# Two first-layer pieces instead of one in each pair of output tiles of an interleaved feed-forward, one Trainium2 core

## The chip, the core and the metric

The kernel runs on one core of a Trainium2 chip. Its engines run side by side, each through its own queue in order: TensorE (matmuls, PE in the profile), VectorE (DVE), ScalarE (ACT), GpSimd (POOL) and SyncE (SP), which issues the loads. The metric is the time of one execution in device microseconds; the time before is the median of three runs.

## The reference

One layer of a hybrid backbone over 1024 tokens of width 1024: a modulated RMSNorm, an input projection into four head groups (convolution, Fourier mixing, neighbourhood attention, state space), an output projection, and then the feed-forward, where the change lies:

```python
def squared_relu_mlp(h, w1, b1, w2, b2):
    return jnp.square(jax.nn.relu(h @ w1 + b1)) @ w2 + b2

hx = modulate(rmsnorm(x_mid, g_norm_mlp[l]), sh2, sc2)
x = x_mid + gt2 * squared_relu_mlp(hx, w_ff1[l], b_ff1[l], w_ff2[l], b_ff2[l])
return rmsnorm(x, g_final)
```

`w_ff1` is 1024 x 4096, `w_ff2` is 4096 x 1024, all in float32.

## The kernel before, in words

Matrices are kept transposed, tokens in two halves of 512. Each float32 operand is split into a high and a low part; a product of 128 x 128 weights with 128 x 512 data takes three matmuls (`mm3w`, line 1470): high by high, high by low, and third the low weights by high. The weights' high part is made by ScalarE, the low part by GpSimd (`w_split`, lines 1455 and 1456).

The 4096 hidden rows are done in 16 units of 256. Both layers use a Strassen-like scheme with seven products where a plain one has eight. For the first layer of unit `u` the seven products are called a11, a12, s1, s2, s3, s4, a22; each has two halves, the 14 *pieces* of six matmuls (`a11.0`, `a11.1` and so on below). They gather in three PSUM banks: qa (a11, s2, s3, a22), qb (s1, s4) and qc (a12). After certain pieces their bank is read: a11.1 copies qa into tile 11, a12.1 adds qc and applies relu and square (`more`, line 1627), s1.1 copies qb into 22, s2.1 copies qa into 12, s3.1 adds qa to 22, s4.1 adds qb to 12 (this add is called `more(12)` below), a22.1 starts 21. Then `sums` (lines 1636 to 1638) and `sum_21` (1645) combine the tiles, and `part` splits them for the second layer (`h_split`: ScalarE the high part, VectorE the low part, line 1488). The sums of the weights for s1 to s4 are made by VectorE (lines 1605, 1607, 1609, 1611).

The second layer of unit `u-1` has four *pairs* of output tiles, each with seven products of three matmuls: a0, a1, b1, b0, c0, c1 and d, where d is run in the next pair, behind its a1. Each product is followed by an add into the result X on VectorE (`add_x`, line 1493). a0, b0, c1 and d of a pair use one bank (fa, of which there are two), one after the other, so each of them waits for the add of the one before; b1 and c0 share fb, a1 uses fc. The weights of a pair are loaded into one of two buffers and combined there by GpSimd (lines 1704 to 1708, three operations right behind the split of `a`, one behind that of `b`); the next load into the buffer is issued with the split of `d`.

The order of the work is written out. `pair_pieces(u - 1, q)` puts pieces of unit `u` between the products of unit `u-1`; three pieces stand ahead of the first pair, and what is left of the 14 comes behind the last, as the unit's tail. `Pieces.emit` walks through that list: at each position it first emits the preparation (split, sums, loads) of what stands up to five positions ahead, then the matmuls, then the callbacks that are due:

```python
            for i, (k, mm, post) in enumerate(self.seq):
                while keys and at[keys[0]] <= i + ahead:
                    key = keys.pop(0)
                    self.w[key] = self.prep[key]()
                mm(self.w[k])
                for d, fn in enumerate(post or ()):
                    self.due.setdefault(i + d, []).append(fn)
                for fn in self.due.pop(i, ()):
                    fn()
```

Within this block TensorE, ScalarE, GpSimd and VectorE run what they are given in that order (`MAN`, line 1447); SyncE's loads and the work outside of the block are placed by a planner. The unit ahead of the paired ones (`u` = 2) is interleaved with `plain_pieces`, which has no such pairs and isn't changed.

Of the kernel before, what the change touches and what calls it, by code (L numbers as in the profile page):

```python
# [49 lines left out]
def body(tc, A, out, dbg=None):  # L50
# [39 lines left out]
    def ps_tile(tag, name, n=512):  # L90
        return cur["pool"].tile([P, n], F32, name=name, tag=tag, bufs=cur["tags"][tag])
# [1359 lines left out]
    def w_split(a):  # L1451

        n = a.shape[1]
        hi, lo = [wf.tile([P, 2, P], F32R, name=s, tag=s, bufs=6)[:, :n] for s in ("w2h", "w2l")]
        S.activation(hi, a, AF.Copy)  # L1455
        G.tensor_tensor(lo, a, hi.bitcast(F32), ALU.subtract)  # L1456
        return hi, lo

    def w1_load(f, i):
        r = wf.tile([P, 4, P], F32, name="w1r", tag="w1r", bufs=4)  # L1460
        SP.dma_start(r, A["w_ff1"][f, :, 4 * i:4 * i + 4])
        return r
# [7 lines left out]
    def mm3w(o, w, i, m, start, stop):  # L1470
        for j, (a_, m_) in enumerate(((w[0], m[0]), (w[0], m[1]), (w[1], m[0]))):
            PE.matmul(o, a_[:, i, :], m_, start=start and j == 0, stop=stop and j == 2, skip_group_check=True)  # L1472

    def f_tile():
        return fin.tile([P, H], F32, name="ft", tag="ft", bufs=4)

    def act(t, f, src=None):

        S.activation(t, t if src is None else src, AF.Relu, bias=CF("b_ff1", f))
        S.activation(t, t, AF.Square)  # L1480

    def h_split(t, extra=False):
        if extra:
            hi, lo = [th_p.tile([P, H], F32R, name=s, tag=s, bufs=3) for s in ("th", "tl")]
        else:
            hi, lo = [fin.tile([P, H], F32R, name=s, tag=s, bufs=4) for s in ("fh", "fl")]
        S.activation(hi, t, AF.Copy)  # L1487
        V.tensor_tensor(lo, t, hi.bitcast(F32), ALU.subtract)  # L1488
        return hi, lo
# [86 lines left out]
    pc = Pieces()  # L1576
# [5 lines left out]
    def q_pieces(u):  # L1582

        ts, d = {}, {}
        units[u] = d
        st = {}

        def load(i):
            if u + 1 < NU2:
                raws.setdefault(u + 1, []).append(w1_load(2 * u + 2 + i // 2, i % 2))  # L1590

        def bank(tag):
            if tag not in st:
                st[tag] = ps_tile(tag, tag)
            return st[tag]

        def prep(name, h):
            def fn():
                a11, a12, a21, a22 = raws[u]
                if h == 0 and name == "s1":  # L1600
                    st["ws"] = wf.tile([P, 4, P], F32, name="ws", tag="ws", bufs=1)
                ws = st.get("ws")
                if h == 0:
                    if name == "s1":
                        ES.tensor_tensor(ws, a21, a22, ALU.add)  # L1605
                    elif name == "s2":
                        ES.tensor_tensor(ws, ws, a11, ALU.subtract)
                    elif name == "s3":
                        ES.tensor_tensor(a21, a11, a21, ALU.subtract)  # L1609
                    elif name == "s4":  # L1610
                        ES.tensor_tensor(ws, a12, ws, ALU.subtract)
                a = {"a11": a11, "a12": a12, "a22": a22, "s3": a21}.get(name, ws)
                w = w_split(a[:, 2 * h:2 * h + 2])
                if h == 0 and name == "s4":
                    for i in range(3):
                        load(i)
                if h == 1 and name == "a22":
                    load(3)
                return w
            return fn  # L1620

        def new(i, bank_):
            ts[i] = f_tile()
            S.copy(ts[i], bank_)  # L1624

        def more(i, bank_, also=None):
            V.tensor_tensor(ts[i], ts[i], bank_, ALU.add)
            if also:
                also()
            act(ts[i], 2 * u + i // 20)  # L1630

        def part(key, i, extra=False):
            d[key] = h_split(ts[i], extra)

        def sums():
            V.tensor_tensor(ts[11], ts[12], ts[11], ALU.subtract)
            V.tensor_tensor(ts[12], ts[22], ts[12], ALU.subtract)
            V.tensor_tensor(ts[22], ts[22], ts[11], ALU.subtract)

        def begin_21():  # L1640
            ts[21] = f_tile()
            act(ts[21], 2 * u + 1, st["qa"])

        def sum_21():
            V.tensor_tensor(ts[21], ts[21], ts[22], ALU.subtract)

        post_q1 = (lambda: new(11, st["qa"]),)
        post_q2 = (lambda: more(11, st["qc"]),)
        post_q5 = (lambda: new(22, st["qb"]),)
        post_q6 = (lambda: new(12, st["qa"]),)  # L1650
        pre_q7 = (lambda: part((0, 0), 11),)
        post_q7 = (lambda: more(22, st["qa"]),)
        if u == NU2 - 1:
            post_q3 = (lambda: more(12, st["qb"]), lambda: part((1, 1), 22), lambda: part((0, 1), 12))
            post_q4 = (begin_21, lambda: part((1, 0), 21))
        else:
            post_q3 = (lambda: more(12, st["qb"], lambda: part((1, 1), 22)), sums)
            post_q4 = (lambda: (begin_21(), part("t1", 11)), lambda: (part((1, 0), 21), part("t2", 22, True)),
                       lambda: (sum_21(), part("t3", 12, True)), lambda: part("t4", 21, True))

        def piece(name, tag, b, start, h, post):
            def mm(w):
                o = bank(tag)
                for k in range(2):
                    mm3w(o, w, k, b[2 * h + k], start and h == 0 and k == 0, h == 1 and k == 1)
            pc.entry((u, name, h), prep(name, h))
            return lambda: pc.add((u, name, h), mm, post if h == 1 else pre_q7 if name == "s3" else None)

        return [piece(*x[:4], h, x[4]) for x in (
            ("a11", "qa", b11, True, post_q1), ("a12", "qc", b21, True, post_q2), ("s1", "qb", c1, True, post_q5),  # L1670
            ("s2", "qa", c2, False, post_q6), ("s3", "qa", c3, False, post_q7), ("s4", "qb", b22, False, post_q3),
            ("a22", "qa", c4, False, post_q4)) for h in range(2)]
# [18 lines left out]
    def pair_pieces(u, q):  # L1691

        late = []
        for p in range(4):
            g = 4 * u + p
            k0, k1 = 2 * p, 2 * p + 1
            bk = {}

            def prep(name, g=g):
                def fn():  # L1700
                    t = raw2[g]
                    w = w_split({"a": t[:, 0:2], "b": t[:, 0:5:4], "c": t[:, 1:3], "d": t[:, 3:4]}[name])
                    if name == "a":
                        EP.tensor_tensor(t[:, 4], t[:, 2], t[:, 3], ALU.add)
                        EP.tensor_tensor(t[:, 2], t[:, 0], t[:, 2], ALU.subtract)
                        EP.tensor_tensor(t[:, 0], t[:, 4], t[:, 0], ALU.subtract)  # L1706
                    elif name == "b":
                        EP.tensor_tensor(t[:, 1], t[:, 1], t[:, 0], ALU.subtract)
                    if name == "d":
                        raw2_load(g + 2)  # L1710
                    return w
                return fn

            for name in "abcd":
                pc.entry((u, p, name), prep(name))

            def prod(name, i, tag, key, hf, k, start, bk=bk, p=p):
                def mm(w):
                    if start:
                        bk[tag] = ps_tile(tag, tag)  # L1720
                    mm3w(bk[tag], w, i, units[u][key], start, True)
                return lambda: pc.add((u, p, name), mm, (lambda: add_x(hf, k, bk[tag]),))

            prod("a", 0, "fa", (0, 0), 0, k0, True)()
            if p == 0:
                q.pop(0)()
            prod("a", 1, "fc", (1, 0), 0, k0, True)()
            if late:
                late.pop()()
            prod("b", 1, "fb", "t1", 1, k1, True)()  # L1730
            prod("b", 0, "fa", "t2", 1, k0, False)()
            q.pop(0)()
            prod("c", 0, "fb", (1, 1), 1, k0, False)()
            prod("c", 1, "fa", "t3", 1, k1, False)()
            late.append(prod("d", 0, "fa", "t4", 0, k1, False))
        q.pop(0)()
        late.pop()()
# [30 lines left out]
    with tc.manual_schedule(engines=MAN):  # L1768
        for u in range(2, NU2):
            q = q_pieces(u)  # L1770
# [164 lines left out]
```

## Time and profile before

| | us |
|---|---|
| median of three runs | 1342.34 (1338.53 to 1344.2) |
| the profiled execution | 1341.13 |
| its span | 1339.0 |
| TensorE busy (matmuls) | 1197.4 (89%) |
| VectorE busy | 1068.4 (80%) |
| GpSimd busy | 808.6 (60%) |
| ScalarE busy | 652.7 (49%) |

The span runs from the first to the last instruction of the profiled execution; its time has 2.1 us more around it. Busy times overlap. The feed-forward's paired units lie between about 770 and 1290 us of the span. TensorE's matmuls are pipelined, so what one takes is read from the distance of two starts, and their shown lengths overlap.

### The profile page before, as it was taken

To read this page: it belongs to the slowest core of one execution; us is meant where nothing else is said; L and a number is where in the kernel's file an instruction comes from. 1 tells how busy PE (TensorE), PEld (TensorE's weight loads), DVE (VectorE), ACT (ScalarE), POOL (GpSimd) and SP (SyncE) were. 2 spreads that over 40 slices of the span, in tenths; PEclk is the share of its full clock that TensorE was granted. 3 is DMA by queue.
4 is the path that set the end of the run, shared out by engine and by line. 5 is a ranking of instruction groups with operands and counts; after the bars stand their busy time and mean duration, and the time that the engine had idled before them with its cause. 6 is when DMAs were issued, how large, how long until landed. Compare 5 with 4: busy or idle time off the path is not lost.

```text
span 1339.0 us, 18718 instructions
## 1 busy us (share of the span) xinstructions
PE 1197.4 (89%) x6188; PEld 965.5 (72%) x6188; DVE 1068.4 (80%) x1636; ACT 652.7 (49%) x1337; POOL 808.6 (60%) x1002
## 2 busy tenths in 40 slices
PE   5889878898865999899999999999999999999996
PEld 3657656777655777777778777777877777777775
DVE  4775999869999768658695579888888888888867
ACT  5254333323446565554664445555545555444555
POOL 3825677372556734015367477777877778787754
PEclk9989898998975999898999999999999999999998
DMA  9455232161153544323121121111211112211113
GB/s 344 142 164 164 81 125 79 47 199 66 51 177 94 175 128 142 109 78 143 32 77 43 40 64 32 48 56 56 63 56 32 52 52 63 64 41 39 56 40 126
DMA packets 75058, 121.77 MB, mean 91 GB/s; under 512 B 16977, under 2 KB 35154, under 8 KB 74962
## 3 DMA queue, kind: packets, MB, share of 16 engines
q1 hardware_dynamic: 62802, 113.24, 26.9%
q10 hardware_dynamic: 12160, 7.34, 1.8%
q8 instruction: 49, 0.80, 0.3%
q14 instruction: 47, 0.39, 0.1%
HBM read 106.68 MB, written 13.88 MB: 90 GB/s over the span
## 4 chain that ended last, share of the span: by engine, by line
PE 48%; DVE 29%; ACT 5%; issue 4%; POOL 4%; DMA 3%; SPq 1%; ACTq 0%; DVEq 0%; POOLq 0%
PE fa L1472 11%; PE qa L1472 6%; PE qb L1472 5%; PE fb L1472 5%; DVE cacc L1015 5%; DVE tl L1488 3%; PE fc L1472 2%; DVE fl L1488 2%; PE f L1472 2%; PE p_t L1270 2%; PE mm L1097 2%; PE mm L1472 2%; DVE Ss L698 2%; DVE Ss L697 1%; DVE X L1493 1%
## 5 line engine op out<-in xcount | busy, mean ns | idle before, releaser
L1456 POOL TENSOR_TENSOR w2l<-w2r,w2h 128x128 fp32r<-128x128 f32 (+1 forms) x232 | 177.4, 766 | 75.3 <-ACT w2h L1455 68.1
L1493 DVE SCALAR_TENSOR_TENSOR X<-fa,gt2c,X 128x512 f32<-128x512 f32 x216 | 159.4, 745 | 13.0 <-PE fa L1472 13.0
L1455 ACT ACTIVATE w2h<-w2r 128x128 fp32r<-128x128 f32 (+1 forms) x232 | 85.8, 387 | 150.8 <-POOL w2r L1706 79.8
L1456 POOL TENSOR_TENSOR w2l<-w1r,w2h 128x256 fp32r<-128x256 f32 x136 | 108.5, 814 | 57.7 <-ACT w2h L1455 34.0
L235 POOL TENSOR_TENSOR wlo<-wraw,whi 128x1024 fp32r<-128x1024 f32 x30 | 75.2, 2508 | 102.0 <-ACT whi L233 82.9
L1493 DVE SCALAR_TENSOR_TENSOR X<-fb,gt2c,X 128x512 f32<-128x512 f32 x108 | 80.5, 745 | 35.4 <-PE fb L1472 35.3
L1456 POOL TENSOR_TENSOR w2l<-ws,w2h 128x256 fp32r<-128x256 f32 x84 | 67.9, 815 | 41.4 <-ACT w2h L1455 40.1
L1015 DVE SCALAR_TENSOR_TENSOR cacc<-cv,wdw,cacc 128x512 f32<-128x512 f32 x92 | 92.3, 1047 | 0.6
L364 PE MATMUL mm<-xl,whi 128*128 128x512 f32 x192 | 81.2, 424 | 3.8 <-DVE xl L220 3.8
L364 PE MATMUL mm<-xh,whi 128*128 128x512 f32 x192 | 77.3, 423 | 7.0 <-ACT xh L218 5.8
L1472 PE MATMUL fa<-th,w2h 128*128 128x512 f32 x156 | 63.2, 405 | 19.7 <-DVE X L1493 19.7
L364 PE MATMUL mm<-xh,wlo 128*128 128x512 f32 x192 | 80.6, 420 | 0.0
L1455 ACT ACTIVATE w2h<-w1r 128x256 fp32r<-128x256 f32 x136 | 53.9, 409 | 47.5 <-DVE w1r L1609 16.5
L1472 PE MATMUL qa<-cb,w2h 128*128 128x512 f32 x224 | 70.7, 397 | 0.7 <-ACT ft L1624 0.7
L1488 DVE TENSOR_TENSOR fl<-ft,fh 128x512 fp32r<-128x512 f32 x64 | 56.9, 906 | 12.8 <-ACT fh L1487 12.7
L1472 PE MATMUL fa<-th,w2l 128*128 128x512 f32 x156 | 61.7, 396 | 0.6 <-POOL w2l L1456 0.6
L1472 PE MATMUL fa<-tl,w2h 128*128 128x512 f32 x156 | 61.5, 394 | 0.0
L1013 POOL TENSOR_TENSOR pacc<-pacc,ptmp 128x512 f32<-128x512 f32 x24 | 37.4, 1559 | 29.8 <-ACT ptmp L1012 29.8
L1455 ACT ACTIVATE w2h<-ws 128x256 fp32r<-128x256 f32 x84 | 33.1, 410 | 42.4 <-DVE ws L1605 20.4
L1472 PEld LDWEIGHTS fa<-th,w2h 128*128 128x128 f32 x156 | 29.3, 188 | 30.8 <-DVE X L1493 25.2
L364 PEld LDWEIGHTS mm<-xh,whi 128*128 128x128 f32 x192 | 38.1, 201 | 18.4 <-ACT xh L218 7.2
L1472 PEld LDWEIGHTS qa<-cb,w2h 128*128 128x128 f32 x224 | 42.0, 188 | 11.2 <-ACT ft L1624 1.1
(788 smaller groups left out, 3945.3 us busy)
## 6 DMA issues: line engine op xcount, KB each, us to landing
w2r<-in_w_ff SPq DMA_DIRECT2D x68, 256.0 KB
wmB<-in_wmodB SPq DMA_DIRECT2D x32, 512.0 KB
w1r<-in_w_ff SPq DMA_DIRECT2D x64, 256.0 KB
wm<-in_wmodA SPq DMA_DIRECT2D x16, 512.0 KB
wraw<-in_w_in SPq DMA_DIRECT2D x12, 512.0 KB
x<-in_xT SPq DMA_DIRECT2D x8, 512.0 KB
wraw<-in_w_out SPq DMA_DIRECT2D x8, 512.0 KB
kr<-k_d SPq DMA_DIRECT2D x16, 256.0 KB
```

Source lines behind the costliest of these rows:

```text
L235: (lo_eng or G).tensor_tensor(lo, raw, hi.bitcast(F32), ALU.subtract)
L364: PE.matmul(o, a_[:, k, :], b_[hf][k], start=k == 0 and i == 0, stop=k == 7 and i == 2)
L698: V.tensor_tensor_scan(Ss[b_, i, g, ::-1], r_[b_], src[b_, g, ::-1], 0.0, ALU.mult, ALU.add)
L1013: G.tensor_tensor(pacc, pacc, t, ALU.add)
L1015: V.scalar_tensor_tensor(acc, x(k), w(k), acc, ALU.mult, ALU.add)
L1097: PE.matmul(o, a_[:, 2 * kk + c, :], b_, start=c == 0 and i == 0, stop=c == 1 and i == 2)
L1270: PE.matmul(po[:, j * 64:j * 64 + 64], ptt[:, i * P:(i + 1) * P], rv, start=i == 0, stop=i == 4, skip_group_check=True)
L1455: S.activation(hi, a, AF.Copy)
L1456: G.tensor_tensor(lo, a, hi.bitcast(F32), ALU.subtract)
L1472: PE.matmul(o, a_[:, i, :], m_, start=start and j == 0, stop=stop and j == 2, skip_group_check=True)
L1488: V.tensor_tensor(lo, t, hi.bitcast(F32), ALU.subtract)
L1493: return V.scalar_tensor_tensor(x, o, gt2(k), x, ALU.mult, ALU.add).ins
```

## The change

In `pair_pieces` one piece now goes between a0 and a1 of every pair, no longer of the first alone. With the one between b0 and c0 each pair has two. So 12 of the 14 pieces stand before the last product, and two are left behind it. Because s3.0 now comes earlier, the split of tile 11 into the operand (0, 0) is called behind s4.0 instead of s3.0.

```diff
-        pre_q7 = (lambda: part((0, 0), 11),)
+        pre_q3 = (lambda: part((0, 0), 11),)
...
-            return lambda: pc.add((u, name, h), mm, post if h == 1 else pre_q7 if name == "s3" else None)
+            return lambda: pc.add((u, name, h), mm, post if h == 1 else pre_q3 if name == "s4" else None)
...
             prod("a", 0, "fa", (0, 0), 0, k0, True)()
-            if p == 0:
-                q.pop(0)()
+            q.pop(0)()
             prod("a", 1, "fc", (1, 0), 0, k0, True)()
```

The order of a paired unit, pairs 0 to 3 (d belongs to the pair before; the head and the tail are alike in what they are):

```
before  head  a11.0 a11.1 a12.0
        0     a0 a12.1 a1   b1 b0 s1.0 c0 c1
        1     a0 a1 d       b1 b0 s1.1 c0 c1
        2     a0 a1 d       b1 b0 s2.0 c0 c1
        3     a0 a1 d       b1 b0 s2.1 c0 c1
        tail  s3.0 d s3.1 s4.0 s4.1 a22.0 a22.1
after   head  a11.0 a11.1 a12.0
        0     a0 a12.1 a1   b1 b0 s1.0 c0 c1
        1     a0 s1.1 a1 d  b1 b0 s2.0 c0 c1
        2     a0 s2.1 a1 d  b1 b0 s3.0 c0 c1
        3     a0 s3.1 a1 d  b1 b0 s4.0 c0 c1
        tail  s4.1 d a22.0 a22.1
```

## Rows read from the trace of the kernel before

**Rows 1.** Stretches of time: limits, length, busy PE, PEld, DVE, ACT, POOL, then PEclk, DMA, GB/s.

```profile
772.92:1290.90 517.98, 499.12 (x2140) 399.25 (x2141) 430.92 (x585) 268.08 (x609) 401.77 (x591) 1.00 0.18 52
```

**Rows 2.** TensorE's waits, 720 to 1260 us: total us, times, longest.

```profile
PE fa L1472 <- DVE X L1493: 18.2, 12, 1.5
```

**Rows 3.** TensorE's timeline around one `b0`: start, length, line, tiles, idle time and its end.

```profile
933.65 0.39 PE L1472 MATMUL fb<-fh,w2l 128*128 128x512 f32 x1
935.55 0.50 PE L1472 MATMUL fa<-th,w2h 128*128 128x512 f32 x1 [1.51 <-DVE X L1493]
...
936.36 0.63 PE L1472 MATMUL qb<-c,w2h 128*128 128x512 f32 x2
...
939.85 0.39 PE L1472 MATMUL fc<-fh,w2h 128*128 128x512 f32 x1
```

**Rows 4.** TensorE's timeline: the `b0` of the first unit and of the third.

```profile
772.92 0.50 PE L1472 MATMUL fa<-th,w2h 128*128 128x512 f32 x1 [1.50 <-DVE X L1493]
...
854.63 0.50 PE L1472 MATMUL fa<-th,w2h 128*128 128x512 f32 x1 [1.52 <-DVE X L1493]
```

**Rows 5.** VectorE's timeline: `more(12)` ahead of the first paired unit, in the third, the last.

```profile
761.26 0.69 DVE L1627 TENSOR_TENSOR ft<-ft,qb 128x512 f32<-128x512 f32 x1 [2.04 <-PE qb L1472]
...
883.38 0.69 DVE L1627 TENSOR_TENSOR ft<-ft,qb 128x512 f32<-128x512 f32 x1 [2.04 <-PE qb L1472]
...
1290.90 0.69 DVE L1627 TENSOR_TENSOR ft<-ft,qb 128x512 f32<-128x512 f32 x1 [2.03 <-PE qb L1472]
```

**Rows 6.** The chain of waits from one `more(12)` to the next `b0`: start, us, what.

```profile
964.52 0.70 DVE ft L1627
...
966.00 0.64 ACT ft L1480
966.66 0.70 DVE ft L1636
...
971.12 1.15 DVE tl L1488
...
973.41 0.76 DVE tl L1488
...
975.48 0.67 DVE X L1493
...
976.20 0.95 PE fa L1472 x3
```

**Rows 7.** GpSimd's timeline behind a `b0`, and in the chain.

```profile
937.90 0.74 POOL L1456 TENSOR_TENSOR w2l<-w2r,w2h 128x256 fp32r<-128x256 f32 x1 [1.11 <-ACT w2h L1455]
...
939.67 0.46 POOL L1706 TENSOR_TENSOR w2r<-w2r 128x128 f32<-128x128 f32 x1
940.09 1.31 POOL L1456 TENSOR_TENSOR w2l<-w2r,w2h 128x128 fp32r<-128x128 f32 x2
...
943.90 0.74 POOL L1456 TENSOR_TENSOR w2l<-w2r,w2h 128x256 fp32r<-128x256 f32 x1 [0.69 <-ACT w2h L1455]
...
967.01 0.94 POOL L1456 TENSOR_TENSOR w2l<-w2r,w2h 128x256 fp32r<-128x256 f32 x1 [1.31 <-ACT w2h L1455]
...
972.82 0.90 POOL L1708 TENSOR_TENSOR w2r<-w2r 128x128 f32<-128x128 f32 x1
```

**Rows 8.** TensorE's timeline at a late low half of weights, pair 2 of the first unit.

```profile
785.11 0.50 PE L1472 MATMUL fa<-th,w2l 128*128 128x512 f32 x1 [0.34 <-POOL w2l L1456]
785.44 0.40 PE L1472 MATMUL fb<-fh,w2h 128*128 128x512 f32 x1
```

**Rows 9.** ScalarE's timeline in the tail ahead of the first paired unit, and behind the last.

```profile
760.01 0.63 ACT L1480 ACTIVATE ft<-ft 128x512 f32<-128x512 f32 x1
760.54 0.71 ACT L1455 ACTIVATE w2h<-w1r 128x256 fp32r<-128x256 f32 x2
761.16 0.62 ACT L1487 ACTIVATE fh<-ft 128x512 fp32r<-128x512 f32 x1
...
1292.92 0.63 ACT L247 ACTIVATE c<-w2r 128x512 fp32r<-128x512 f32 x1 [2.63 <-DMA w2r<-in_w_ff]
```

## The prediction

> **What bounds the kernel now.** I read the stretches of time first, then the waits of TensorE, then TensorE's own timeline around the longest wait, then the chain of waits through that place, then GpSimd's timeline beside it. From 772.92 to 1290.90 us the feed-forward's paired units run: TensorE is busy 499 of 518 us, VectorE 431, GpSimd 402 [rows 1]. That looks like a full TensorE. Its waits are one kind: 12 times in the window about 1.5 us for an add into X [rows 2]. The timeline shows it: `b0`, the fourth product of a unit's first pair, starts 1.90 us after the matmul before it, where 0.23 is usual [rows 3]. `b0` accumulates on the bank that `a0` filled, so it waits for `a0`'s add.
>
> I cut each unit in two. A *stretch* runs from that `b0` to the end of `s4.1`, marked by the VectorE add that reads bank qb (`more(12)`). A *chain* runs from there to the next unit's `b0`. In the stretch TensorE sets the pace: from 936.36 to 939.85 lie 15 matmuls, 0.2327 us each [rows 3]; the shortest stretch, 854.63 to 883.38, takes 28.75 us for 123 of them [rows 4, 5]. In the chain TensorE does not: it has 45 matmuls to run, some 10 us, and the chain takes 11.68 us (964.52 to 976.20), nearly all on VectorE, with two activations on ScalarE near its start [rows 6]. From 772.92 to 1290.90 there are 13 stretches and 12 chains, so the 13 stretches sum to 517.98 - 12 x 11.68 = 377.8, a mean of 29.06 [rows 4, 5].
>
> **The change part by part.** Pairs 1, 2 and 3 each get a second piece, between `a0` and `a1`. The pieces move forward: `s1.1` from after pair 1's `b0` to before its `a1`, `s2.0` from pair 2 to pair 1, and so on; `s3.1`, `s4.0`, `s4.1` leave the tail. No matmul, add or split is added or dropped.
>
> *Stretch, matmuls.* Between `s4.1` and the next `b0` there were 45 matmuls; now the last product `d` also falls behind `s4.1`, so 48. The stretch loses 3 x 0.2327 = 0.70 us, 13 times: -9.1. This is certain as far as the stretch is TensorE's.
>
> *Chain, the moved add.* With `d` behind `s4.1` its add moves too. Callbacks due at one position run in the order in which they were registered; `sums` was registered by `s4.1` for the next position, before `d` registers its add there. So VectorE does `more(12)`, the split of (1,1), waits for ScalarE's square, does the three sums, and then `d`'s add, in front of everything that the next `a0`'s add stands behind. It costs 0.67 [rows 6]. VectorE does idle ahead of the sums, until the square ends at 966.64: `more(12)` ends at 965.22, the split of (1,1) takes 0.7 to 1.1, so 0.3 to 0.7 us are free [rows 6]. The add can't use them, because the order puts it later. Bounds: 0 if it hid in that wait, 0.67 if not.
>
> *Chain, GpSimd.* VectorE's two-input work in the chain is slow: the split at 971.12 took 1.15 us, the one at 973.41 took 0.76; GpSimd was busy from 967.01 to 973.72 [rows 6, 7]. They slow each other. In the new order the weights of `a12.0` of the next unit are prepared after ScalarE's square, no longer before it, because that preparation is queued five positions ahead and `s4.1` now stands one position earlier. So one more 0.74 us GpSimd operation falls into the chain. Against that, `d`'s add reads PSUM, and GpSimd ran at its short durations (0.74 and 0.46) beside such adds at 937.90 to 940.13 [rows 7], so it catches up 0.67 us of its work meanwhile. Net I take -0.07, between -0.1 and +0.74. The chain grows by 0.67 - 0.07 = 0.60, 12 times: +7.2.
>
> The Trainium skill (SBUF — State Buffer, Who interferes with whom) calls this an exclusive lock for the whole instruction, where the loser fully blocks. The stretched pairs of rows agree that it isn't free; taken strictly, the extra preparation would be paid in full, which is the third rival.
>
> *Stretch, `s1.1`'s weights.* This is the new wait. `s1.1` stands where pair 1's `a1` stood, 4.30 us after `b0` (939.85 - 935.55) [rows 3]. Its third matmul is the first that reads the low half of the weights: 4.30 + 0.46 = 4.76. GpSimd makes that half in program order after the preparation of pair 1's `a`, a low half and three combinations: started at 937.90, the last combination is at 939.67, and the next operation starts at 940.09 [rows 7], 4.54 after `b0`. This sequence can't start earlier: its ScalarE half stands behind the activation that follows the late `a0` add. The low half of 0.74 us is therefore ready at 5.28, and TensorE starts at 5.32, 0.56 late. A restart after such a wait costs 0.10 more (785.11 to 785.44 is 0.33) [rows 8]. So +0.66, 13 times: +8.6. Bounds: 0 if GpSimd were half a microsecond earlier, 0.9 if VectorE work beside it stretches the operation to 1.15. Behind that matmul stands all of TensorE's queue. VectorE's sum for `s2`, which overwrites what `s1.1`'s preparation reads, waits until 5.28 as well; the next add behind it, `a1`'s, has its product only at about 7.2, so nobody waits for that. In the old order `d` stood at that place in GpSimd's queue and was needed at 5.4, after its operation.
>
> *Stretch, other waits.* 13 x (29.06 - 28.75) = 4.0 us are lost in the old stretches, by preparations that come late in pairs 2 and 3, such as the one at 785.11 [rows 8]. A pair now holds 33 matmuls (7.7 us) instead of 27 (6.3), while GpSimd gets one more low half of 0.74. Pair 2's `a` began at 943.90, 8.35 after `b0` [rows 7]; 0.74 later, with its own 0.7, three combinations (1.6) and a low half, `s2.1` is ready at 12.1. Its third matmul is the 54th after `b0`: 53 x 0.2327 + 0.1 + 0.66 = 13.1, so 1.0 us is to spare. I take 3.0 of the 4.0 as gone: -3.0, between -4.0 and 0.
>
> *Moved wait of (0,0).* Its split goes from after `s3.0` to after `s4.0`, for otherwise it would wait for a buffer that pair 3's `a0` still reads. In paired units VectorE has room there. In the unit ahead of them, which has no pairs, `s4.0` and `s4.1` follow each other, and ScalarE does the activation of `s3.1` first: its square starts at 760.01, two weight splits at 760.54, the split of (1,1) at 761.16 [rows 9]. The split of (0,0) now comes between those two: done at about 761.5, VectorE's half about 762.15, and only then `more(12)`, which was at 761.26 [rows 5]. Once +1.0, between 0 and 1.4.
>
> *DMA.* The load behind each pair's `d` is issued when GpSimd has read that buffer; for pair 3 that is later, but the next reader is a pair away. The first-layer loads move forward. I cost both at 0. In the last unit ScalarE waits 2.63 us at 1290.3 for a second-layer load [rows 9], ahead of the final stage; another place for it would cost or give about that much. I take 0, between -1.9 and +2.6.
>
> Sum: -9.1 + 7.2 + 8.6 - 3.0 + 1.0 = +4.7 on the profiled execution's 1341.13 us (span 1339.0): 1345.8. The median of the three runs is 1342.34, 1.2 above that execution, and I lean toward it by a little: **1346 us**.
>
> **Rivals.**
> 1. *The pieces fill in and nothing is given back.* `d`'s add hides in the wait for the square and `s1.1` finds its weights: -9.1 - 3.0 = -12.1, 1329 us. For it: VectorE idles 0.3 to 0.7 us in the chain. Against it: the written order and GpSimd's time of 4.54, which was the same within 0.02 us in all 13 units. The Trainium skill (Perfetto Trace Analysis, Optimization Strategy) says that regimes with different limits may gain by being interleaved; a VectorE-bound tail and a TensorE-bound run of products are such, and this is that case. Chance 0.12.
> 2. *The gain turns into a longer wait, and no more.* `s1.1` is in time, but the chain grows: -9.1 + 7.2 - 3.0 + 1.0 = -3.9, 1337 us. For it: the 0.56 is a difference of two times of 5 us, and the low half need only come from an earlier place in GpSimd's queue. Chance 0.20.
> 3. *GpSimd takes VectorE's time in the chain.* The extra low half stretches VectorE by its full 0.74 instead of being made up beside the add: 0.67 + 0.74 = 1.41 per chain, 12 x (1.41 - 0.60) = +9.7 over the forecast, 1355 us. It makes the kernel slower as soon as the chain grows by more than the 0.70 that the stretch loses. For it: the 1.15 us durations; against: GpSimd's short durations beside PSUM adds. Chance 0.18.
>
> **How the numbers follow.** The forecast, slower by 4.7, has 0.50; its own range is 1339 to 1351 (chain 0.2, `s1.1` 0.2, final stage 2 us either way). About 0.5% (6.7 us) is what a measurement of this kernel can tell from no change. Faster by more than that: only rival 1, 0.12. Slower by more: rival 3 with 0.18 and the upper quarter of the forecast, 0.12, together 0.30. Within: 0.58. The range 1334 to 1355 leaves out rival 1 and the end of rival 3.
>
> **What would show it.** In TensorE's waits of the changed kernel: the wait of `b0` for X still about 1.5 us, 13 times, and a new wait of `s1.1` (bank qb) for GpSimd's low half, about 0.5 us, 13 times. From `more(12)` to the next `b0` 12.2 to 12.4 us, with an add into X behind the third sum; stretches of about 28.8 us; the period of a unit about 41.0 (40.75 on average now). The forecast is wrong if `b0` no longer waits (then TensorE binds and the kernel is near rival 1), if `s1.1` starts without a wait (rival 2), or if the split durations in the chain are all at 1.15 (rival 3).

## The result, and the profile after

The changed kernel is slower: 1349.11 us (1345.88 to 1353.46, six runs) against 1339.13 us for the kernel before, beside it on the same chips. The ratio is 1.0070, with an interval of 1.0044 to 1.0096; measured a second time it was 1.0080 (1.0061 to 1.0099). The profiled execution has a span of 1345.4 us, 6.4 more than [rows 1]'s kernel.

The paired units by stretches of time (columns as in [rows 1]): 525.7 us where 518.0 stood, with TensorE and VectorE busy for nearly the same time as before.

```profile
773.80:1299.47 525.67, 501.41 (x2137) 400.62 (x2138) 430.28 (x584) 260.30 (x608) 393.76 (x590) 1.00 0.17 51
```

TensorE's waits in the paired units: the old wait of `b0` for X is still there [rows 2], and a new one has come, of `s1.1` on bank qb for GpSimd's low half. It stands in 12 of the 13 units: in the first, TensorE ran at its lower level of 1.2 GHz for some 3 us behind `b0` (granted clock 0.50 from 774.70 to 777.60) and reached `s1.1` after its weights were there. Of the further profiles below, the one with such a fall has 12 of these waits too, the two without have 13.

```profile
PE fa L1472 <- DVE X L1493: 21.3, 13, 1.9
PE qb L1472 <- POOL w2l L1456: 4.8, 12, 0.4
```

TensorE's timeline of one unit shows it in place (compare [rows 3]). `b0` starts at 1022.62, `s1.1` 4.31 us later, and its third matmul 5.33 us after `b0`; two matmuls at 0.23 would have brought it at 4.78. It starts 0.55 late and the next one 0.34 after it.

```profile
1022.62 0.50 PE L1472 MATMUL fa<-th,w2h 128*128 128x512 f32 x1 [1.62 <-DVE X L1493]
...
1026.93 0.62 PE L1472 MATMUL qb<-c,w2h 128*128 128x512 f32 x2
1027.95 0.50 PE L1472 MATMUL qb<-c,w2l 128*128 128x512 f32 x1 [0.40 <-POOL w2l L1456]
1028.29 0.62 PE L1472 MATMUL qb<-c,w2h 128*128 128x512 f32 x2
```

GpSimd's timeline of that unit: the low half of `s1.1` (1027.16) stands behind `a`'s (1024.97) and the last combination, and ends at 1027.89, 5.27 after `b0`. In [rows 7] the operation at that place was `d`'s.

```profile
1024.97 0.74 POOL L1456 TENSOR_TENSOR w2l<-w2r,w2h 128x256 fp32r<-128x256 f32 x1 [1.10 <-ACT w2h L1455]
...
1026.75 0.46 POOL L1706 TENSOR_TENSOR w2r<-w2r 128x128 f32<-128x128 f32 x1
1027.16 0.73 POOL L1456 TENSOR_TENSOR w2l<-ws,w2h 128x256 fp32r<-128x256 f32 x1
```

The chain of waits from `more(12)` to the next `b0`, to hold against [rows 6]: 1010.13 to 1022.62, 12.49 us instead of 11.68. The add into X at 1015.26 is `d`'s, behind the third sum. The third sum (line 1638) took 1.11 us, where it took 0.84 before.

```profile
1010.13 0.70 DVE ft L1627
...
1011.61 0.64 ACT ft L1480
...
1012.28 0.70 DVE ft L1636
...
1014.15 1.11 DVE ft L1638
1015.26 0.66 DVE X L1493
1015.92 1.62 DVE fl L1488 x2
1017.54 1.15 DVE tl L1488
...
1019.84 0.76 DVE tl L1488
...
1021.91 0.67 DVE X L1493
...
1022.62 0.96 PE fa L1472 x3
```

Ahead of the paired units, ScalarE's timeline and then VectorE's ([rows 9] and [rows 5]): the split of (0,0) at 760.77 stands between the square and the split of (1,1), VectorE waits 2.28 us for it, and `more(12)` follows only at 762.15. From the start of ScalarE's square that is 2.22 us, where it was 1.25.

```profile
759.93 0.63 ACT L1480 ACTIVATE ft<-ft 128x512 f32<-128x512 f32 x1
...
760.77 0.62 ACT L1487 ACTIVATE fh<-ft 128x512 fp32r<-128x512 f32 x1
...
761.60 0.62 ACT L1487 ACTIVATE fh<-ft 128x512 fp32r<-128x512 f32 x1
```

```profile
761.42 0.81 DVE L1488 TENSOR_TENSOR fl<-ft,fh 128x512 fp32r<-128x512 f32 x1 [2.28 <-ACT fh L1487]
762.15 0.68 DVE L1627 TENSOR_TENSOR ft<-ft,qb 128x512 f32<-128x512 f32 x1
```

### The profile page after: what moved, and what is told of

It is laid out like the page before. It is cut to its first block, busy times and chain, and to the rows that moved or that the text cites. A ratio compares the mean times of both kernels' runs of the same rounds, so it can differ in the third digit from the quotient of the medians.

```text
span 1345.4 us, 18677 instructions
## 1 busy us (share of the span) xinstructions
PE 1197.9 (89%) x6188; PEld 965.5 (72%) x6188; DVE 1064.6 (79%) x1636; ACT 645.4 (48%) x1337; POOL 803.8 (60%) x1002
## 4 chain that ended last, share of the span: by engine, by line
PE 47%; DVE 30%; ACT 5%; issue 4%; POOL 4%; DMA 3%; SPq 1%; ACTq 0%; DVEq 0%; POOLq 0%
PE fa L1472 10%; PE qa L1472 6%; PE qb L1472 5%; PE fb L1472 5%; DVE cacc L1015 5%; DVE tl L1488 3%; PE fc L1472 2%; DVE X L1493 2%; DVE fl L1488 2%; PE p_t L1270 2%; PE mm L1097 2%; PE f L1472 2%; PE mm L1472 2%; DVE Ss L698 2%; DVE Ss L697 1%
## 5 line engine op out<-in xcount | busy, mean ns | idle before, releaser
L1456 POOL TENSOR_TENSOR w2l<-ws,w2h 128x256 fp32r<-128x256 f32 x84 | 62.0, 739 | 64.7 <-ACT w2h L1455 63.4
L1493 DVE SCALAR_TENSOR_TENSOR X<-fc,gt2c,X 128x512 f32<-128x512 f32 x56 | 41.9, 747 | 25.4 <-PE fc L1472 25.2
L1488 DVE TENSOR_TENSOR fl<-ft,fh 128x512 fp32r<-128x512 f32 x64 | 49.7, 793 | 11.5 <-ACT fh L1487 11.5
```

The costliest lines, as they stand in the source:

```text
L1493: return V.scalar_tensor_tensor(x, o, gt2(k), x, ALU.mult, ALU.add).ins
```

## The experiments

I cut each trace into stretches and chains as the prediction does. Times are ratios to the kernel before, run on the same chip, with 95% intervals.

| kernel | ratio | interval | stretch, us | chain, us |
|---|---|---|---|---|
| before | 1 | | 28.75 to 29.97 | 11.68 |
| changed | 1.0070 | 1.0044 to 1.0096 | 28.84 | 12.49 |
| changed, again | 1.0080 | 1.0061 to 1.0099 | 28.84 | 12.49 |
| `s1.1` behind `a1` | 1.0008 | 0.9996 to 1.0020 | 28.17 | 12.49 |
| add first | 1.0046 | 1.0029 to 1.0064 | 28.83 | 12.25 |
| three mends | 0.9987 | 0.9968 to 1.0006 | 28.17 | 12.25 |
| preparation early | 1.0030 | 1.0012 to 1.0047 | 28.83 | 12.14 |
| four mends | 0.9951 | 0.9929 to 0.9972 | 28.17 | 12.01 |
| before, split of (0,0) moved | 1.0120 | 1.0095 to 1.0144 | 29.94 | 11.65 |
| before, more GpSimd work | 1.0034 | 1.0018 to 1.0051 | 28.86 | 12.07 |

Stretch and chain are medians over the units of the profiled execution, but for the range in the first row.

**The changed kernel again.** No edit.

> The changed kernel once more, as the yardstick for the others. Theory A (two costs of known size: d's add in the chain, s1.1's wait for its low half): stretches of 28.8 us, chains of 12.5, and a time 6 to 10 us over the kernel before. Theory C (the time beyond the 6 us that the first profile showed comes from TensorE running at its half clock behind some of the longer waits, as it did from 774.6 to 777.6 us in that profile): this profile shows such a drop at other places or at none, with stretches that differ by 1 us or more where there is one.

Stretches of 28.83 or 28.84 in all 13 units, chains of 12.49, ratio 1.0080. The first unit, 29.72 us in the first profile, took 28.84 here, so that one was an accident of the execution: TensorE had run there at 0.43 us a matmul, the lower level.

**`s1.1` behind `a1`.** Only pair 1's extra piece is moved by one product.

```diff
-            q.pop(0)()
+            if p != 1:
+                q.pop(0)()
             prod("a", 1, "fc", (1, 0), 0, k0, True)()
+            if p == 1:
+                q.pop(0)()
```

> The changed kernel, but in pair 1 the extra piece stands behind a1 instead of ahead of it, so that s1.1's low half is needed 0.7 us later. Theory A: the wait for GpSimd at s1.1 is gone, a stretch is 28.2 instead of 28.8 us, 13 x 0.6 = 8 us less than the changed kernel. Rival (the wait only moves: the next low half in GpSimd's queue, d's, is late instead): stretches stay at 28.7 to 28.9, and the time is that of the changed kernel within 1 us. The chain stays at 12.5 in both.

TensorE's timeline of one unit: `b0` at 1017.45, `a1` (bank fc) 4.29 later, `s1.1` at 4.97, and its third matmul at 5.44 without a wait. In the paired units TensorE now waits for X alone.

```profile
1017.45 0.50 PE L1472 MATMUL fa<-th,w2h 128*128 128x512 f32 x1 [1.62 <-DVE X L1493]
...
1021.74 0.39 PE L1472 MATMUL fc<-fh,w2h 128*128 128x512 f32 x1
...
1022.42 0.63 PE L1472 MATMUL qb<-c,w2h 128*128 128x512 f32 x2
1022.89 0.40 PE L1472 MATMUL qb<-c,w2l 128*128 128x512 f32 x1
```

The stretch is 0.67 us shorter, 13 x 0.67 = 8.7, and the ratio falls from 1.0080 to 1.0008, by 9.7 us on 1341, which agrees within the two intervals. The wait was worth what the prediction put on it, and moving one piece by one product removes it with nothing late in its place.

**Add first.** The sums are called one position later, so that VectorE does `d`'s add before them.

```diff
-            post_q3 = (lambda: more(12, st["qb"], lambda: part((1, 1), 22)), sums)
+            post_q3 = (lambda: more(12, st["qb"], lambda: part((1, 1), 22)), lambda: None, sums)
```

> The changed kernel, but the three sums are called one position later, so that d's add stands ahead of them in VectorE's queue, where VectorE waits for ScalarE's square. Theory A: the chain falls from 12.5 to 11.8 to 11.95 us, 12 x 0.6 = 7 us less than the changed kernel; stretches stay at 28.8. Rival B (the chain grew because one more GpSimd preparation lies in it, and the add matters only as a free window for GpSimd): GpSimd loses that window, the chain stays at 12.2 or above, at most 3 us less.

The chain falls by 0.24 only: theory A missed, the rival came nearer. The chain of waits shows what stands behind the add:

```profile
1014.67 2.75 PE qa L1472 x12
...
1017.44 0.70 ACT ft L1479
...
1018.16 0.64 ACT ft L1480
1018.80 0.53 ACT fh L1487
...
1019.35 1.57 DVE fl L1488 x2
```

Now the split at 1019.35 waits for ScalarE, and ScalarE for `a22`, which `d` has pushed back by 0.70 us. The add had covered that wait. And VectorE's last two splits of the chain (from 1022.85) take 2.09 us in its timeline, where the changed kernel has 1.55: GpSimd, which the add no longer leaves alone there, works beside them to the end.

**Three mends.** Both edits, and in the unit ahead of the paired ones (0,0) is split behind s3.0 again.

```diff
-... else pre_q3 if name == "s4" else None)
+... else pre_q3 if name == ("s3" if u == 2 else "s4") else None)
```

> Both edits, and in the unit ahead of the paired ones the split of (0,0) is back behind s3.0. Theory A: the costs add up, stretch 28.2, chain 11.9, a unit 40.1 us, the first more(12) 0.9 us earlier: 16 us less than the changed kernel and 7 less than the kernel before. Rival B: chain at 12.2 or above, 40.4 or more per unit, about 4 us less than before at best. If the two costs share one cause, the gain of both is that of one, 8 us, and the time is that of the kernel before.

The two costs add up in the trace (28.17 and 12.25, 40.42 a unit), and from ScalarE's square ahead of the units to the first `more(12)` it is 1.28 us again. The time is 1.7 us below the kernel before, an interval that includes no change (0.9968 to 1.0006), and not 7 us below. Of the 5.3 us missed (some 2.5 either way), 12 x (12.25 - 11.9) = 4.2 are the chain's.

**Preparation early.** The weights of `a12.0` are prepared six positions ahead.

```diff
-                while keys and at[keys[0]] <= i + ahead:
+                while keys and at[keys[0]] <= i + ahead + (keys[0][1:] == ("a12", 0)):
```

> The changed kernel, but the weights of the next unit's a12.0 are prepared one position earlier, ahead of the activation behind more(12), so that their low half falls before GpSimd's part in the chain. Theory A as the prediction had it (d's add costs 0.67, the preparation nothing on balance): chains stay at 12.4 to 12.5 us. Theory B as the run with the add first suggests (its removal gave 0.24, so 0.57 of the 0.81 us belong to the preparation): chains of 11.9 to 12.1, 5 to 7 us less than the changed kernel. Stretches of 28.8 in both.

The chain is 12.14, 0.35 less: the preparation, for which the prediction had -0.07 on balance, gives back more when it alone is taken out than the add does. The gain isn't ScalarE's: its square ends 2.11 us after `more(12)` in both kernels, while VectorE's third sum is back at 0.84. The gain falls short of theory B's 0.57, and the ratio, 1.0030, is 0.50% under the changed kernel's second measurement.

**Four mends.** The three mends and the early preparation together.

> The kernel with the three mends, and the preparation of a12.0 one position earlier as well. Theory B: with the add and the preparation both out of the chain it is back at its old 11.7 us, stretches 28.2, a unit 39.9 us against 40.75 before: 6 us less than the three mends, 7 to 10 less than the kernel before. Theory A: chains stay at 12.25 and the time is that of the three mends.

The chain is 12.01, not 11.7, and a unit 40.2 us. The ratio is 0.9951 (0.9929 to 0.9972): this version beats both kernels, by 6.6 us against the one before. Of the chain's 0.81 us the two edits give back 0.24 and 0.35 alone and 0.48 together; the other 0.33 stand at one place. VectorE's timeline of one unit, then ScalarE's square:

```profile
964.67 0.69 DVE L1627 TENSOR_TENSOR ft<-ft,qb 128x512 f32<-128x512 f32 x1 [0.62 <-PE qb L1472]
965.47 1.10 DVE L1488 TENSOR_TENSOR fl<-ft,fh 128x512 fp32r<-128x512 f32 x1
966.49 0.74 DVE L1493 SCALAR_TENSOR_TENSOR X<-fa,gt2c,X 128x512 f32<-128x512 f32 x1
967.15 0.67 DVE L1636 TENSOR_TENSOR ft<-ft 128x512 f32<-128x512 f32 x1
```

```profile
966.15 0.63 ACT L1480 ACTIVATE ft<-ft 128x512 f32<-128x512 f32 x1
```

The first sum starts 2.48 us after `more(12)`, where it started 2.14 after it before (966.66 - 964.52) [rows 6]. The square is done at 966.78, but `d`'s add still runs. With the preparation early, the split of (1,1) (965.47) takes 1.10 us, where it takes 0.69 in the kernel with the add first, and starts 0.80 us after `more(12)` instead of 0.60. So the add no longer fits into the wait for the square. From the first sum to the next `b0` it is 9.5 us, as before the change.

**The split of (0,0) moved alone**, in the kernel before.

```diff
-        pre_q7 = (lambda: part((0, 0), 11),)
+        pre_q3 = (lambda: part((0, 0), 11),)
...
-... else pre_q7 if name == "s3" else None)
+... else pre_q3 if name == "s4" else None)
```

> The kernel before, with only the call of (0,0)'s split moved from behind s3.0 to behind s4.0 and the pieces where they were, so that s4.0 and s4.1 stand next to each other in every unit. Theory A: what happened once, in the unit ahead of the pairs, happens in each: VectorE's half waits for ScalarE, more(12) starts about 0.9 us late, 14 x 0.9 = 12 us more than before. Rival (ScalarE has room in the paired units, the 0.9 us belonged to the unit without pairs): within 2 us of the kernel before.

Every unit now shows on VectorE what the changed kernel showed once ahead of them:

```profile
1012.28 0.81 DVE L1488 TENSOR_TENSOR fl<-ft,fh 128x512 fp32r<-128x512 f32 x1 [2.29 <-ACT fh L1487]
1013.01 0.67 DVE L1627 TENSOR_TENSOR ft<-ft,qb 128x512 f32<-128x512 f32 x1
```

The median stretch grows by 1.0 us to 29.94, and in four units it is 30.8 to 31.3 us, for a reason given in the last section; the time is 16 us over the kernel before, where theory A had 12. In the changed order, where products stand between `s4.0` and `s4.1`, VectorE waits 0.5 us at most for a split's high part in the paired units.

**More GpSimd work in the chain**, in the kernel before.

```diff
         def sums():
+            for _ in range(2):
+                G.tensor_tensor(ident, ident, ident, ALU.mult)
```

> The kernel before with two more GpSimd operations of 128 x 128 (0.46 to 0.53 us each on their own) in each unit's chain, which multiply a 0/1 matrix by itself and change nothing. It prices GpSimd's work in the chain by itself. Theory A (what VectorE loses is made good elsewhere): chains stay at 11.7. Theory B: the chain grows by about 0.8 us for each us of GpSimd work, the price that 0.57 for a low half of 0.70 gives, so to 12.4 to 12.6 us, and the time by 12 x 0.8 = 9 to 10 us. A strict lock that VectorE always loses: by the full 1.0, 12.7.

The chain grows by 0.39 us (11.68 to 12.07), half of what theory B gave. In its chain of waits the two VectorE operations that start beside the short ones take 0.80 and 0.81 us, where 1.15 and 1.14 stood before. The last split comes after a gap of 0.29 us, for which the trace shows no wait, and takes 1.22, where it took 0.68:

```profile
1020.06 0.80 DVE tl L1488
1020.87 0.81 DVE ft L1647
...
1022.73 1.22 DVE tl L1488
```

So VectorE pays GpSimd's work in part: 0.39 us for two operations of 0.46, some 0.4 us per us, not all and not nothing. The two added operations themselves took 1.65 us together. TensorE waits 0.95 us for a late low half in this chain too, but `b0` still waits 0.66 us for X behind it, so VectorE sets its start.

The Trainium skill (SBUF — State Buffer, Who interferes with whom) has the shared port pair as an exclusive lock: who issues first has it for the whole instruction, and the other blocks. That both engines slow down agrees; that VectorE pays the whole of it, as the expectation's strict reading has it, does not.

**Further profiles** of both kernels, to find what the traces leave unexplained in the time.

> One more profile of the changed kernel. The two so far put 6.2 us on it, the timed runs 8 to 13. Theory C (half clock behind the longer waits): the paired units take more than 525 us here, with stretches 1 us longer where TensorE runs at half clock. Theory D (the remainder lies ahead of the feed-forward, where nothing was changed, and varies from one execution to the next): the paired units take 525 us within 1, and the first more(12) comes anywhere from 761 to 767 us.

> One more profile of the kernel before. Theory D: the paired units take 518 us as in the first profile, and the first more(12) comes anywhere from 760 to 766 us. Theory C says the same of the units, for its waits are shorter, and that the first more(12) stays at 761.

> A further profile of the changed kernel, as the one before it: units at 525 and a varying start by theory D, units above 525 by theory C.

> A further profile of the kernel before: units at 518 by both theories, a varying start by theory D.

The sum from the first `b0` to the last `more(12)` is 524.8 to 525.7 us in four profiles of the changed kernel and 517.2 to 518.0 in three of the one before. The first `more(12)` comes at 762.15, 761.80, 763.87 and 756.38 us in the changed kernel, at 761.26, 763.59 and 764.18 before. Theory D holds in the main: the part ahead, which the change touches by 1 us at most, varies by 8 us between executions, and 756.38 lies even below the 761 to 767 that were expected. Theory C's fall of the clock is there in one of the two further profiles of the changed kernel, and is worth 0.9 us. From the first `more(12)` to the end the spans take 583.6 and 577.4 us on average, 6.2 more; with the 0.97 us ahead of it (2.22 - 1.25) the traces account for 7.1 us, 0.53%. That lies within the first interval of the time and just below the second (0.61%). What would make up the rest isn't settled.

## Why the prediction was right, and where its sizes were off

The direction, the places and the range were right; the size was short. Forecast were 1346 us and +4.7 on the profiled execution. That execution came out 6.2 us longer (6.4 in the span), and the timed median at 1349.11. By the ratio the change costs 9.4 us (5.9 to 12.9), about twice the forecast and beyond 0.5%, the case that had 0.30. That the sums of the table lie as near as 4.7 and 6.4 is in part luck: the chain and the first unit were 3.4 us too low, the final stage 2.2 too high. The signs that the prediction named came out, but for the chain, at 12.49 us where it had 12.2 to 12.4, and the period of a unit, 41.33 where it had 41.0.

| step | forecast, us | measured in the traces |
|---|---|---|
| matmuls out of the stretch, and fewer late weights | -9.1 - 3.0 = -12.1 | 13 x (28.17 - 29.07) = -11.7 |
| `s1.1`'s wait | +8.6 | 13 x (28.84 - 28.17) = +8.7 |
| chain | 12 x 0.60 = +7.2 | 12 x (12.49 - 11.68) = +9.7 |
| the unit ahead | +1.0 | 2.22 - 1.25 = +1.0 |
| final stage | 0 | 45.93 - 48.10 = -2.2 |
| first unit at the lower clock | none | 29.72 - 28.84 = +0.9 |
| sum | +4.7 | +6.4 |

*Matmuls, late weights, `s1.1`.* As forecast, and shown by experiment: the low half of `s1.1` came at 5.27 (forecast 5.28), and taking the wait away gave it back. The waits of pairs 2 and 3 for low halves [rows 8] are gone.

*Chain.* This is the step that failed in its parts. The prediction split it into 0.67 for `d`'s add and -0.07 for the preparation of `a12.0`, "net". In the trace of one unit the add does cost what was forecast, 0.66. What failed is GpSimd's term: instead of -0.07 it is 0.27 for the third sum, less 0.12 for the two splits behind the add (1.62 instead of 1.74), +0.15. The prediction gave the extra GpSimd work a full refund during the add. The trace shows a refund of one operation (line 1705 ran in 0.46 us there), while the third sum rose from 0.84 to 1.11, beside a low half where it had stood beside a short combination. First VectorE before, then GpSimd in the changed kernel:

```profile
968.54 0.84 DVE L1638 TENSOR_TENSOR ft<-ft 128x512 f32<-128x512 f32 x1
```

```profile
1013.53 1.19 POOL L1456 TENSOR_TENSOR w2l<-w2r,w2h 128x256 fp32r<-128x256 f32 x1
...
1015.66 0.46 POOL L1705 TENSOR_TENSOR w2r<-w2r 128x128 f32<-128x128 f32 x1
```

The chain's growth was put 0.21 us too low, 2.5 us in all. Taking a cost out gives back another amount than its place in the chain: the preparation alone 0.35, the add alone 0.24, because behind the add another wait stood ready, `a22`'s way through ScalarE, which moved back by the same product.

*Final stage.* In this execution a little beyond its bounds (-1.9 to +2.6). TensorE waited 2.33 us at 1295.92 before, behind ScalarE's late load [rows 9]. In the changed kernel it waited 0.27 us at that place, and 0.7 us of the old wait are filled by `d` of the last unit. TensorE's timeline before, then in the changed kernel:

```profile
1295.92 1.12 PE L1472 MATMUL f<-fh,c 128*128 128x512 f32 x3 [2.33 <-ACT fh L1487]
1296.84 0.63 PE L1472 MATMUL f<-fl,c 128*128 128x512 f32 x1
...
1300.25 0.40 PE L1472 MATMUL f<-fl,c 128*128 128x512 f32 x1
```

```profile
1303.13 0.72 PE L1472 MATMUL f<-fh,c 128*128 128x512 f32 x2 [0.27 <-ACT fh L1487]
...
1304.73 0.39 PE L1472 MATMUL f<-fl,c 128*128 128x512 f32 x1
...
1306.60 0.39 PE L1472 MATMUL f<-fl,c 128*128 128x512 f32 x1
```

The fourth matmul of that stage comes 0.7 us earlier after the last `more(12)` than before (5.26 against 5.94), the twelfth 2.2 us earlier (7.13 against 9.35). The other 1.5 are the clock: before, TensorE ran at the lower level behind that wait (granted clock 0.50 from 1296.90 to 1300.20), and in the changed kernel it didn't. The prediction had no such term. Other profiles of the changed kernel have 46.9 to 47.1 us in the final stage, those of the one before 48.1 to 48.2, so about 1.1 us are usual.

*The rivals.* That the pieces fill in and nothing is given back (1329 us) fell: the four mends come nearest, at 0.9951. That the gain turns into a longer chain alone (1337) is the order of the kernel with `s1.1` behind `a1`, but its ratio is 1.0008, not 0.997: its chain costs 9.7 us and not 7.2, and the final stage of its profile took 49.4 us, 1.3 more than before. That GpSimd takes its full 0.74 of VectorE's time fell short: the chain grew by 0.81, not 1.41.

## What to carry to other kernels

A piece of work moved forward in a written order takes its preparation along: before filling a gap on the bottleneck, find at what time each helper engine can have the operands ready at the new place, in that engine's own order. And look at what the move leaves behind: here three pieces left the tail, but one product and its add slipped from ahead of the last dependency to behind it, onto the path that set the period. When one cost on such a path is removed, look for the wait that it had covered before expecting all of it back.

## What the runs showed of the hardware that was not expected

TensorE's clock fell behind waits only a little longer than the usual ones. In the kernel with the (0,0) split moved, `b0` waits 1.82 to 1.86 us in every unit, and in four of 13 the matmuls behind it then run at 0.43 us, the lower level of 1.2 GHz, for about 3 us (granted clock 0.50 from 815.80 to 819.10 in the first of them):

```profile
814.28 0.50 PE L1472 MATMUL fa<-th,w2h 128*128 128x512 f32 x1 [1.82 <-DVE X L1493]
...
817.05 0.63 PE L1472 MATMUL fb<-fh,w2h 128*128 128x512 f32 x1
817.47 0.63 PE L1472 MATMUL fb<-fl,w2h 128*128 128x512 f32 x1
```

The changed kernel shows it in the first unit alone, in two of four profiles, both behind waits of 1.87. In the other two the first unit's waits of 1.88 and 1.82 brought no fall, and neither did the 48 waits of the later units, 1.61 to 1.63 each. With the first units of the three kernels that still had the moved split there (`s1.1` behind `a1`, add first, preparation early), 8 of 20 waits of 1.82 to 1.88 were followed by a fall. Behind the longer waits in the final stage of the kernel before, 2.33 to 2.39, it came in all three profiles. The length of one wait isn't all of it: in the final stage of the kernel with `s1.1` behind `a1` the clock fell behind three waits of 0.69, 0.36 and 0.83 close together, and behind 0.43, 0.36 and 0.83 in the second profile of the changed kernel it did not. What decides isn't shown. Such a fall behind `b0` costs 0.9 to 1.5 us on top of the wait.
